# A two-layer latent backbone on one core: five instead of four tiles of the input projection multiplied while their input is still being made

## The chip, the core and the metric

The kernel runs on one core of a Trainium2 chip. Its engines each take their instructions in the order in which they stand in the program: PE (the matrix engine, with PEld for its weight loads), DVE (vector), ACT (scalar), POOL, and SP, which here only issues transfers. The metric is the time of one execution in microseconds, smaller is better. Results of PE go to PSUM, which has eight banks of 128 x 512 numbers; everything else lies in SBUF or, through transfers, in DRAM.

## What is computed

Two layers over 256 context tokens and 256 latent tokens, 1024 wide. What matters here is the start of the first layer: both streams are modulated (scaled and shifted by two vectors that come out of a product of the condition with `mod_w`), and the result goes through one wide projection `w_in`. Part of its output, `rw`, is mixed with its neighbours in time and feeds a recurrent scan.

```python
for l in range(DEPTH):
    sh1, sc1, g1, sh2, sc2, g2 = split((silu(c) @ mod_w[l] + mod_b[l]), 6)
    cq, ckv, kr, ch, cb, cc, rw, gt = split(modulate(x, sh1, sc1) @ w_in[l], IN_SPLITS)
    ...
    # rwkv_features: part is rw
    part = part + (0.5 * (up[:, :-2] + up[:, 2:]) - part) * mu
    r, k, v, wd, ad, gd = split(part, ...)
    kk = kkf * rsqrt(max(sum(square(kkf)), 1e-24))     # kkf = heads(k * k_k)
    ...
    # scan over the tokens, both directions; attention; gated merge; FFN
```

## The kernel before

Each product in full precision is made of three matmuls on split operands (`mm3`, L238 to L240: high by high, high by low, low by high), 128 x 512 each. Since the inner size is 1024, one output tile of `w_in` (128 features by all 512 tokens) takes 8 x 3 = 24 matmuls and one PSUM bank. `w_in` has 57 such tiles. Fifteen of them are the `rw` part, here called tiles 0 to 14: 0 and 1 feed the decay and the learning rate of the scan, 2 to 5 are its keys.

`start` makes the modulated input of the first layer in eight pieces k = 0 to 7 (one for each 128 of the 1024 channels): it loads `mod_w`, multiplies it (`mod`, L259, and `mod_out`, L266, into the banks `p_m`), transposes x (L1295, bank `p_i`), scales and shifts on DVE (L1299) and splits into `xh` and `xl` (ACT and DVE, L245 and L246). While the pieces come, the first `M_START` tiles of `w_in` are already multiplied. Tile m is loaded and split (`wload`, L193 and L194) at piece m, catches up on pieces 0 to m, and then takes part in each later piece. Tiles 0 and 1 use the two banks `pg`, the others the banks `p_w`:

```python
if k < M_START:
    ws.append(wload(A["win"][0, M_RW + k], [128, 8, 128], pl=ip, tag="w", nb=4 * M_START))
    acc.append(pg() if k < 2 else pr("w", M_START - 2))
...
for m in range(len(ws)):
    for kk in range(k + 1) if m == k else (k,):
        mm3(acc[m], ws[m][0](kk), ws[m][1](kk), xh[:, kk], xl[:, kk], kk == 0, kk == 7)
```

When piece 7 is done, `feature(m, acc[m])` takes each tile out of its bank: ACT copies it to `pp` (L480), POOL adds the neighbours into `nb` (L483), ACT scales `pp` (L484), DVE combines both (L485), and SP stores `nb` to DRAM as `feat` (L491). `pp` and `nb` share a ring of four buffers. Tiles 0 and 1 are then loaded again for the scan (`tw`, L967) and split on ACT (`wa`, L245). The later tiles are multiplied one after the other by `gemm_in` into three banks in turn and taken out the same way. The four key tiles are loaded back as `kn` (L537, through the same ring of four buffers), squared on ACT (L937), and summed on PE (`p_y<-bones,kn`, L945).

The program is written in one order and a scheduler in the language's framework then reorders the instructions of every engine before the kernel is built. The order that each engine gets is fixed from then on. So a change in one place may move instructions elsewhere.

Of the kernel before, what the change touches and what calls it, by code (L numbers as in the profile page):

```python
# [46 lines left out]
R_WD, R_AD, R_K, R_R, R_V, R_GD = 0, 1, 2, 6, 10, 14  # L47
NM_IN = 57

M_START = 4  # L50
N_EARLY = (24, 24)
N_CONV = (2, 1)
BC = 4
# [23 lines left out]
def body(ctx: ExitStack, tc: tile.TileContext, A: dict, out: bass.AP, dbg=None, upto=None):  # L77
# [12 lines left out]
    def pg():  # L90

        if extra[0]:
            extra[1] = (extra[1] + 1) % (extra[0] + 2)
            if extra[1] < extra[0]:
                return psp[0].tile([128, 512], F32, tag="x", name="pg", bufs=extra[0])
        return psg.tile([128, 512], F32, tag="g", name="pg")

    def pr(tag, bufs=1):
        return psp[0].tile([128, 512], F32, tag=tag, name="p_" + tag, bufs=bufs)
# [76 lines left out]
    def wload(src, shape, pl=None, tag=None, nb=None, to=None):  # L176

        w, n = shape[-1], int(np.prod(shape[1:]))
        raw = ring.tile([128, 1024], F32, tag="raw", name="raw", bufs=3)
        sp.dma_start(out=raw[:, :n].rearrange("p (a b) -> p a b", b=w), in_=src)  # L180
        his, los = [], []
        for i, o in enumerate(range(0, n, 512)):
            m = min(512, n - o)
            if to:
                hi, lo = (t[:, o:o + m] for t in to)
            else:
                p = pl or ring
                hi = p.tile([128, 512], F32R, tag=tag or "hi", name="hi", bufs=nb or 4)[:, 0:m]
                lo = p.tile([128, 512], F32R, tag=tag or "lo", name="lo", bufs=nb or 4)[:, 0:m]
            r = raw[:, o:o + m]  # L190
            cnt[0] += 1
            e = pool if share[0] and cnt[0] % share[0] == 0 else dve
            act.copy(out=hi, in_=r)  # L193
            e.tensor_tensor(out=lo, in0=r, in1=hi.bitcast(F32), op=ALU.subtract)  # L194
            his.append(hi)
            los.append(lo)

        def part(ts):
            return lambda k: ts[k * w // 512][:, k * w % 512:k * w % 512 + w]

        return part(his), part(los)
# [35 lines left out]
    def mm3(ps, wh, wl, xh, xl, first, last):  # L237
        pe.matmul(ps, wh, xh, start=first, stop=False, skip_group_check=True)  # L238
        pe.matmul(ps, wh, xl, start=False, stop=False, skip_group_check=True)  # L239
        pe.matmul(ps, wl, xh, start=False, stop=last, skip_group_check=True)  # L240

    def split(src, hi, lo, scale=None):

        if scale is None:
            act.copy(out=hi, in_=src)  # L245
            dve.tensor_tensor(out=lo, in0=src, in1=hi.bitcast(F32), op=ALU.subtract)  # L246
        else:
            act.mul(out=hi, in_=src, mul=scale)
            dve.scalar_tensor_tensor(out=lo, in0=src, scalar=scale, in1=hi.bitcast(F32), op0=ALU.mult,
                                     op1=ALU.subtract)  # L250
# [197 lines left out]
    def layer(l, xh=None, xl=None, pre=()):  # L448
# [16 lines left out]
        with ExitStack() as rws:  # L465
# [42 lines left out]
            if l == 0:  # L508
                xh, xl = start(feature)
                m0 = M_START  # L510
            rp = rws.enter_context(tc.tile_pool(name=f"rw{l}", reuse_waits="tile", bufs=1))
# [760 lines left out]
    def start(feature):  # L1272

        xh, xl = new_xm()
        with tc.tile_pool(name="ini", bufs=1, reuse_waits="tile") as ip, banks("psi"):
# [9 lines left out]
            for k in range(8):  # L1285
# [15 lines left out]
                split(xf, xh[:, k], xl[:, k])  # L1301
# [3 lines that stand above are left out]
                if k == X_AT:  # L1305
# [5 lines left out]
# [3 lines that stand above are left out]
            for m in range(M_START):  # L1314
                feature(m, acc[m])
# [78 lines left out]
```

## Time and profile before

| | |
|---|---|
| time, three runs | 1870.13, 1872.61, 1875.64 us; median 1872.61 us |
| the profiled execution | 1882.8 us, of which its span 1881.0 us |
| granted TensorE clock over the span | 0.969 |
| PE busy | 1795.3 us (95%), 13556 instructions |
| DVE / ACT / POOL busy | 1087.1 / 842.4 / 547.3 us |
| transfers | 380.45 MB, mean 202 GB/s |

The profile lists each instruction with its start, its length and, in brackets, how long its engine had been idle before it and which instruction ended that wait. Matmuls overlap each other by their filling and draining, so the distance from one start to the next, not the length, is what one costs. "Granted clock" is the share of TensorE's full clock (2.4 GHz) that the chip gave; 0.5 is 1.2 GHz.

### The profile page before, as it was taken

To read this page: it belongs to the slowest core of one execution; us is meant where nothing else is said; L and a number is where in the kernel's file an instruction comes from. 1 tells how busy PE (TensorE), PEld (TensorE's weight loads), DVE (VectorE), ACT (ScalarE), POOL (GpSimd) and SP (SyncE) were. 2 spreads that over 40 slices of the span, in tenths; PEclk is the share of its full clock that TensorE was granted. 3 is DMA by queue.
4 is the path that set the end of the run, shared out by engine and by line. 5 is a ranking of instruction groups with operands and counts; after the bars stand their busy time and mean duration, and the time that the engine had idled before them with its cause. 6 is when DMAs were issued, how large, how long until landed. Compare 5 with 4: busy or idle time off the path is not lost.

```text
span 1881.0 us, 35386 instructions
## 1 busy us (share of the span) xinstructions
PE 1795.3 (95%) x13556; PEld 1477.6 (79%) x13556; DVE 1087.1 (58%) x2012; ACT 842.4 (45%) x1830; POOL 547.3 (29%) x558
## 2 busy tenths in 40 slices
PE   7999999999989998999999998999999999989997
PEld 5777877777768767877888887777788886869996
DVE  4357724873367787543444346168874368855665
ACT  2557333823245453444444213386523365535552
POOL 1356113611133221454343015244302132420001
PEclk9998999999989999999999999988899999989999
DMA  8443534343495326799999425775586573576573
GB/s 339 135 143 107 163 131 155 105 156 124 166 313 161 120 74 217 261 370 345 344 335 357 134 89 177 236 233 157 177 262 212 185 267 121 175 289 225 182 240 106
DMA packets 182698, 380.45 MB, mean 202 GB/s; under 512 B 33984, under 2 KB 89344, under 8 KB 182528
## 3 DMA queue, kind: packets, MB, share of 16 engines
q1 hardware_dynamic: 179552, 369.59, 58.1%
q10 hardware_dynamic: 2976, 8.59, 1.3%
q8 instruction: 107, 1.75, 0.4%
q14 instruction: 63, 0.52, 0.1%
HBM read 301.53 MB, written 76.58 MB: 201 GB/s over the span
## 4 chain that ended last, share of the span: by engine, by line
PE 73%; DVE 9%; DMA 9%; ACT 5%; issue 3%; POOL 1%; SPq 0%; ACTq 0%; POOLq 0%; DVEq 0%
PE pg L238 10%; PE pg L239 10%; PE pg L240 10%; PE p_f L238 9%; PE p_f L240 9%; PE p_f L239 8%; DMA raw<-in_win_dram 3%; PE p_G L1066 2%; PE p_G L755 2%; DVE lo L194 1%; PE pg L259 1%; PE p_y L776 1%; ACT hi L193 1%; DMA raw<-in_ffn_w_dram 1%; DVE sq L1106 1%
## 5 line engine op out<-in xcount | busy, mean ns | idle before, releaser
L194 DVE TENSOR_TENSOR lo<-raw,hi 128x512 fp32r<-128x512 f32 (+1 forms) x408 | 317.1, 787 | 361.8 <-ACT hi L193 358.5
L193 ACT CAST hi<-raw 128x512 fp32r<-128x512 f32 x478 | 286.5, 616 | 424.6 <-PE p_f L239 97.0
L238 PE MATMUL pg<-xh,hi 128*128 128x512 f32 (+1 forms) x912 | 335.7, 370 | 12.1 <-ACT pp L480 3.7
L240 PE MATMUL pg<-xh,lo 128*128 128x512 f32 (+1 forms) x912 | 329.4, 361 | 0.2
L239 PE MATMUL pg<-xl,hi 128*128 128x512 f32 (+1 forms) x912 | 327.8, 359 | 0.4 <-DVE xl L246 0.4
L238 PE MATMUL p_f<-x2h,hi 128*128 128x256 f32 (+1 forms) x688 | 232.9, 338 | 7.2 <-ACT hi L193 7.2
L240 PE MATMUL p_f<-x2h,lo 128*128 128x256 f32 (+1 forms) x688 | 231.9, 337 | 1.1 <-DVE lo L194 1.0
L239 PE MATMUL p_f<-x2l,hi 128*128 128x256 f32 (+1 forms) x688 | 231.5, 336 | 0.0
L238 PEld LDWEIGHTS pg<-xh,hi 128*128 128x128 f32 x912 | 180.2, 198 | 45.3 <-issue 9.1
L240 PEld LDWEIGHTS pg<-xh,lo 128*128 128x128 f32 x912 | 180.7, 198 | 25.8 <-issue 2.0
L239 PEld LDWEIGHTS pg<-xl,hi 128*128 128x128 f32 x912 | 180.8, 198 | 21.9 <-DVE xl L246 1.0
L194 POOL TENSOR_TENSOR lo<-raw,hi 128x512 fp32r<-128x512 f32 x70 | 93.2, 1331 | 343.2 <-ACT hi L193 306.5
L238 PEld LDWEIGHTS p_f<-x2h,hi 128*128 128x128 f32 x688 | 131.5, 191 | 22.5 <-ACT hi L193 9.4
L240 PEld LDWEIGHTS p_f<-x2h,lo 128*128 128x128 f32 x688 | 131.4, 191 | 15.8 <-DVE lo L194 2.6
L239 PEld LDWEIGHTS p_f<-x2l,hi 128*128 128x128 f32 x688 | 131.5, 191 | 12.7
L231 POOL TENSOR_TENSOR wlo<-wraw,whi 128x512 fp32r<-128x512 f32 x70 | 92.7, 1345 | 123.7 <-ACT whi L230 123.5
L334 POOL TENSOR_TENSOR rs<-rs,mhalf 128x1 f32<-128x1 f32 x12 | 8.8, 730 | 352.8 <-DVE rs L353 352.8
L1050 POOL TENSOR_TENSOR FM<-ta,di 64x256 f32<-64x256 f32 x64 | 57.4, 897 | 37.3 <-ACT FM L1044 21.6
L661 POOL TENSOR_TENSOR acc<-acc,gts 128x512 f32<-128x512 f32 (+1 forms) x32 | 38.7, 1217 | 79.9 <-DVE gts L659 67.3
L259 PE MATMUL pg<-raw,cs 128*32 128x128 f32 x1024 | 53.7, 299 | 2.0 <-DMA raw<-in_modw_dram 1.7
L1106 DVE TENSOR_TENSOR sq<-sq,iv 128x31 f32<-128x31 f32 (+15 forms) x124 | 50.6, 408 | 3.4
L1066 PE MATMUL p_G<-AR,FM 64*128 64x128 f32 x384 | 51.0, 290 | 1.1 <-DVE AR L1074 1.0
(393 smaller groups left out, 3599.2 us busy)
## 6 DMA issues: line engine op xcount, KB each, us to landing
raw<-in_modw_dram SPq DMA_DIRECT2D x96, 512.0 KB, 4.8
raw<-in_w_dram SPq DMA_DIRECT2D x88, 512.0 KB, 5.2
raw<-in_win_dram SPq DMA_DIRECT2D x79, 512.0 KB, 4.3
raw<-in_ffn_w_dram SPq DMA_DIRECT2D x44, 512.0 KB, 3.7
wraw<-in_win_dram SPq DMA_DIRECT2D x35, 512.0 KB, 6.1
win<-whi SPq DMA_DIRECT2D x35, 512.0 KB, 5.8
win<-wlo SPq DMA_DIRECT2D x35, 512.0 KB, 5.3
hi<-win SPq DMA_DIRECT2D x70, 256.0 KB, 4.0
```

The source lines that it names most:

```text
L193: act.copy(out=hi, in_=r)
L194: e.tensor_tensor(out=lo, in0=r, in1=hi.bitcast(F32), op=ALU.subtract)
L231: pool.tensor_tensor(out=lo[:, s], in0=raw[:, s], in1=hi[:, s].bitcast(F32), op=ALU.subtract)
L238: pe.matmul(ps, wh, xh, start=first, stop=False, skip_group_check=True)
L239: pe.matmul(ps, wh, xl, start=False, stop=False, skip_group_check=True)
L240: pe.matmul(ps, wl, xh, start=False, stop=last, skip_group_check=True)
L259: pe.matmul(ps[32 * (k % 4):32 * (k % 4) + 32, 0:128], cs[:, o:o + 32], raw[:, k], start=(j == 0 and k < 4), stop=(k >= 4), skip_group_che ...
L661: pool.tensor_tensor(out=a, in0=a, in1=g, op=ALU.add)
L755: pe.matmul(ps[:, 0:nk], qT[:, h, qt * 128:(qt + 1) * 128], kT[:, h, 0:nk], start=True, stop=True)
L1050: pool.tensor_tensor(out=FM[r, :, k0:k0 + 64], in0=rc(ta[r]), in1=rc(Pi[r]), op=ALU.mult)
L1066: pe.matmul(ps[:, j * 128:j * 128 + ncol], FM[r, j], AR[z][r, e, hp, j, 0:ncol], start=True, stop=True)
L1106: dve.tensor_tensor(out=Ti[:, j + 1:32, 0:w], in0=Ti[:, j + 1:32, 0:w], in1=tv, op=ALU.subtract)
```

## The change

One constant is raised, which makes `start` load, split and multiply tile 4 at piece 4 as well. Its accumulator is a third `p_w` bank, so that all eight banks are taken in `start` (two `pg`, two `p_m`, one `p_i`, three `p_w`). The weights' ring in `start` grows from 16 to 20 buffers, and `gemm_in` has one tile fewer to do.

```diff
-M_START = 4
+M_START = 5
```

The set of instructions stays the same: all engines run as many of each kind as before, and only one copy out of PSUM reads a `p_w` instead of a `pg` bank. The order does change. Every engine's order differs in many places in the mixers of the first layer, in a few in its feed-forward part and at the start of the second layer, and then not at all.

The first place is on PE, in piece 4. `pg_310`, `pg_367`, `p_w_424` and `p_w_487` are the banks of tiles 0 to 3, `p_m` those of the modulation. Before, the last tile's matmuls are followed by the modulation of the next piece, and then piece 5 begins:

```order
L239 MATMUL p_w_487<-xl_253,hi_483 128x512
L240 MATMUL p_w_487<-xh_252,lo_484 128x512
L266 MATMUL p_m_558<-pick_78,modrow_579 128x4
L259 MATMUL p_m_607<-raw_608,cs_77 32x128 x5
L259 MATMUL p_m_607<-raw_618,cs_77 32x128 x8
L259 MATMUL p_m_656<-raw_657,cs_77 32x128 x8
```

Now tile 4 (`p_w_556`) catches up there; of its fifteen matmuls the first three and the last three are shown:

```order
L240 MATMUL p_w_487<-xh_252,lo_484 128x512
L238 MATMUL p_w_556<-xh_252,hi_548 128x512
L239 MATMUL p_w_556<-xl_253,hi_548 128x512
L240 MATMUL p_w_556<-xh_252,lo_549 128x512
...
L238 MATMUL p_w_556<-xh_252,hi_552 128x512
L239 MATMUL p_w_556<-xl_253,hi_552 128x512
L240 MATMUL p_w_556<-xh_252,lo_553 128x512
L266 MATMUL p_m_584<-pick_78,modrow_605 128x4
```

Fifteen matmuls moved ahead of the modulation of pieces 5 to 7, and three more go into each of these pieces.

The second place is on ACT, where the first tiles of `gemm_in` leave PSUM. `pp_838`, `pp_881` and `pp_964` belong to tiles 5, 6 and 7, the four `kn` to the key tiles, and `tw`, `di` and `PC` to the scan's decay. Before:

```order
L484 ACTIVATE pp_838<-pp_838,hv0_83 128x2x256
L480 COPY pp_881<-pg_856 128x2x256
L1026 ACTIVATE tw_1323<-tw_1323,ones_70 128x256
L193 CAST hi_1024<-raw_1022 128x512
L1030 ACT_TABLE_LOAD
L1030 ACTIVATE di_1329<-tw_1323 128x256
L484 ACTIVATE pp_881<-pp_881,hv0_83 128x2x256
L1031 ACTIVATE tw_1323<-tw_1323 128x256
L1032 COPY PC_1298<-tw_1323 128x4
L193 CAST hi_1028<-raw_1022 128x512
L937 ACTIVATE kn_889<-kn_889,sv_74 128x2x256
L937 ACTIVATE kn_902<-kn_902,sv_74 128x2x256
```

Now:

```order
L484 ACTIVATE pp_838<-pp_838,hv0_83 128x2x256
L480 COPY pp_881<-pg_856 128x2x256
L193 CAST hi_1028<-raw_1022 128x512
L484 ACTIVATE pp_881<-pp_881,hv0_83 128x2x256
L937 ACTIVATE kn_889<-kn_889,sv_74 128x2x256
L937 ACTIVATE kn_902<-kn_902,sv_74 128x2x256
L193 CAST hi_1067<-raw_1065 128x512
L193 CAST hi_1071<-raw_1065 128x512
L937 ACTIVATE kn_911<-kn_911,sv_74 128x2x256
L937 ACTIVATE kn_920<-kn_920,sv_74 128x2x256
L480 COPY pp_964<-pg_939 128x2x256
```

The decay's instructions went behind the keys' squares; tile 7 still leaves its bank behind all four squares. On PE the first sum over a key tile (L945) stands, before, behind 121 matmuls of `gemm_in` and six small ones (`p_c<-wa,uhl`) counted from the end of `start`; now behind 100 and three.

The third place is on PE at the end of the first layer's mixers, where the last pieces of the modulation (L259, L266) are made between the scan's read-out (L1233 and L1248 are transposes, L1267 the read-out's gate) and the merge (`pg<-br,hi`). Before:

```order
L1233 MATMUL p_y<-ident,Yf 128x128 x4
L266 MATMUL pg<-pick,modrow 128x4
L1267 MATMUL p_G<-sg,lw 128x256
L276 MATMUL pg<-ident,modT_81 16x128
L259 MATMUL pg<-raw,cs 32x128 x24
L266 MATMUL pg<-pick,modrow 128x4
L259 MATMUL pg<-raw,cs 32x128 x16
L266 MATMUL pg<-pick,modrow 128x4
L1248 MATMUL p_y<-ident,gn 128x128 x4
L259 MATMUL pg<-raw,cs 32x128 x8
L1233 MATMUL p_y<-ident,Yf 128x128 x4
L1267 MATMUL p_G<-sg,lw 128x256
```

Now:

```order
L259 MATMUL pg<-raw,cs 32x128 x16
L1248 MATMUL p_y<-ident,gn 128x128 x4
L259 MATMUL pg<-raw,cs 32x128 x8
L266 MATMUL pg<-pick,modrow 128x4
L1233 MATMUL p_y<-ident,Yf 128x128 x4
L259 MATMUL pg<-raw,cs 32x128 x8
L266 MATMUL pg<-pick,modrow 128x4 x2
L259 MATMUL pg<-raw,cs 32x128 x16
L266 MATMUL pg<-pick,modrow 128x4
L238 MATMUL pg<-br,hi 128x512
```

Between the last tile of `gemm_in` and the merge there stand one L1248 group, one L1233 group and two L1267 fewer than before; they come later, among the merge's matmuls.

## Rows read from the trace of the kernel before

**Rows 1.** Stretches: length; busy (count) PE, PEld, DVE, ACT, POOL; PEclk; DMA share; GB/s.

```profile
30.00:43.76 13.76, 13.51 (x120) 9.72 (x119) 8.14 (x16) 4.99 (x10) 2.71 (x2) 1.00 0.81 317
43.76:55.47 11.71, 11.71 (x110) 9.96 (x108) 6.07 (x18) 2.98 (x6) 0.44 (x1) 1.00 0.22 59
...
93.00:100.00 7.00, 6.93 (x28) 5.72 (x29) 4.11 (x5) 2.98 (x6) 5.60 (x6) 0.76 0.17 47
```

**Rows 2.** PE in order of time: start, length, instruction.

```profile
43.76 0.28 PE L266 MATMUL p_m<-pick,modrow 128*128 128x4 f32 x2
...
55.47 0.39 PE L238 MATMUL pg<-xh,hi 128*128 128x512 f32 x1
...
60.91 0.39 PE L238 MATMUL pg<-xh,hi 128*128 128x512 f32 x1
...
71.88 0.38 PE L238 MATMUL p_c<-wa,uhl 64*128 64x256 f32 x1
...
72.78 0.50 PE L238 MATMUL pg<-xh,hi 128*128 128x512 f32 x1
```

**Rows 3.** Chain that ended last: start, us, what.

```profile
58.30 2.54 DMA feat<-nb
60.86 2.18 DMA tw<-feat
...
64.90 2.44 DMA feat<-nb
67.36 1.99 DMA tw<-feat
...
71.23 4.69 DMA feat<-nb
...
79.52 4.12 DMA kn<-feat
...
83.66 0.73 ACT kn L937
```

**Rows 4.** ACT in order of time.

```profile
54.36 0.59 ACT L480 COPY pp<-pg 128x512 f32<-128x512 f32 x1 [2.53 <-PE pg L240]
...
92.43 0.59 ACT L480 COPY pp<-pg 128x512 f32<-128x512 f32 x1 [1.31 <-POOL pp L479]
```

**Rows 5.** PE in order of time, around the keys' sums.

```profile
84.44 1.05 PE L945 MATMUL p_y<-bones,kn 128*128 128x2 f32 x8 [0.26 <-ACT kn L937]
...
93.06 0.79 PE L238 MATMUL pg<-xh,hi 128*128 128x512 f32 x1 [1.29 <-ACT pp L480]
...
96.22 0.49 PE L239 MATMUL pg<-xl,hi 128*128 128x512 f32 x1
```

**Rows 6.** Transfer issues: count, KB each, median us to landing.

```profile
feat<-nb SPq DMA_DIRECT2D x25, 256.0 KB, 3.1
...
kn<-feat SPq DMA_DIRECT2D x4, 256.0 KB, 4.1
```

**Rows 7.** PE in order of time, later waits of the first layer.

```profile
248.11 0.44 PE L1188 MATMUL p_c<-Zs,LB 64*64 64x64 f32 x2 [2.54 <-ACT LB L1138]
...
536.79 1.12 PE L1233 MATMUL p_y<-ident,Yf 128*128 128x128 f32 x4 [2.13 <-ACT Yf L1251]
...
550.01 1.12 PE L1233 MATMUL p_y<-ident,Yf 128*128 128x128 f32 x4 [0.58 <-ACT Yf L1251]
```

**Rows 8.** Stretches around those waits, columns as in rows 1.

```profile
241.00:250.00 9.00, 6.46 (x151) 4.92 (x153) 1.07 (x2) 5.72 (x11) 1.26 (x1) 0.81 0.34 119
250.00:259.00 9.00, 9.00 (x72) 6.71 (x64) 2.24 (x4) 2.49 (x6) 0.00 (x0) 0.81 0.42 147
...
536.00:542.00 6.00, 4.63 (x57) 3.31 (x57) 3.33 (x8) 3.16 (x9) 0.00 (x0) 0.72 0.83 266
542.00:548.00 6.00, 3.61 (x40) 2.62 (x40) 2.43 (x7) 1.43 (x5) 1.98 (x1) 0.63 0.98 370
548.00:554.00 6.00, 5.42 (x44) 3.63 (x43) 3.85 (x9) 3.36 (x9) 1.52 (x2) 0.52 1.03 381
```

## The prediction

> **What bounds the kernel now.** I first read the stretches of the start, because the change moves work into it. From 43.76 us, where the fifth tile is put in, to 55.47 us PE is busy for all of the 11.71 us, and in the 13.76 us before it for all but 0.25 [rows 1]. Next I read PE in order of time: the matmuls of tile 4 now begin at 55.47, right behind the last matmul of `start`, and end at 60.91 where tile 5 begins [rows 2]. So PE has no hole there, neither where the tile goes to nor where it is taken from. Transfers are no limit in that stretch (DMA share 0.22 [rows 1]), and the load of tile 4's weights stands at the same place of SP's queue as before.
>
> Then the chain that ended last, read from 58 to 85 us. It doesn't run over PE there: tile 0 is stored to DRAM (2.54 us) and read back (2.18), tile 1 stored (2.44) and read back (1.99), tile 3 stored (4.69), and the first key tile read back (4.12), with short pieces of ACT and DVE between [rows 3]. It begins with the copy of tile 0 out of its bank at 54.36 [rows 4] and ends in the square at 83.66, which the first sum over a key tile waits for on PE. That sum starts at 84.44, after a wait of 0.26 us [rows 5]: chain and PE arrive together. Then PE waits 1.29 us at 93.06 for tile 7 to leave its bank [rows 5], and runs slow for a while.
>
> **The change, part by part.** *The matmuls.* Tile 4 has 24 matmuls; 60.91 - 55.47 = 5.44 us, 0.227 each [rows 2]. They leave one full stretch and enter another, so they gain 0. (TensorE: Matmul & The Clock Gate of the Trainium skill, section "Wait — 56ns, not 53.3ns?", gives 215.7 ns for such a matmul at the full clock; the trace's 0.227 is 5% above it. If all of that were room to be had, it would be 24 x 0.011 = 0.3 us of an estimate, no term here.) The two casts and two subtractions of tile 4's weights were already made in piece 5 before, so ACT and DVE only have those of tile 6 more there, in time that PE's fifteen extra matmuls cover (DVE is busy for 6.07 of 11.71 us, ACT for 2.98 [rows 1]). The fifth bank costs nothing: the next user of that bank is the scan, after 100 us.
>
> *Tile 0 leaves later.* Between 43.76 and tile 0's last matmul PE now does 15 matmuls in piece 4, 3 each in pieces 5 and 6, and 1 in piece 7: 22 x 0.227 = 5.0 us. The copy at 54.36 [rows 4] comes at 59.4, and with it the whole chain of stores and loads, since it is made of latencies and not of PE's work. Left alone it would bring the first squared key 5.0 us later, ready at 84.4 + 5.0 = 89.4.
>
> *PE comes just as early.* By the order the first key sum stands behind 100 matmuls of `gemm_in` and 3 small ones, counted from the end of `start`, which comes at 60.91 now. 100 x 0.227 = 22.7, and half of the 0.90 us between 71.88 and 72.78 that six small ones take [rows 2], make 84.05. Before, it came at 84.18. So the key sum, which waited 0.26 us, would wait up to 5.3. How much of the 5.0 the chain makes up is not in the trace, so I bound it: if the store of 4.69 and the load of 4.12 [rows 3] both took the 2.2 us of the short reloads, it would save 4.4, and the wait is 1.0; if nothing, 5.3. I take the middle by the medians: the store's is 3.1 and the key load's is 4.1 [rows 6], so only the store becomes shorter, by 1.6. The wait becomes 84.4 + 5.0 - 1.6 - 84.05 = 3.7 us. Behind that sum on PE stand tiles 9 and 10, with their operands ready; nobody can pass.
>
> DMA: Bandwidth & Descriptors of the Trainium skill, section "Anatomy of one DMA — SWDGE (gpsimd) path", puts a transfer at some 2.0 us plus its bytes over 436 GB/s. For 256 KB that is an estimate of 2.6 us; the stores of 2.54 and 2.44 agree with it, the 4.69 and the 4.12 do not [rows 3]. By it both long ones would be 2.6, the chain would make up 3.6, and the sum below would be 0.4 instead of 2.4. I go by the medians.
>
> *The clock after the wait.* From 93.06 to 96.22 seven matmuls took 3.16 us instead of 1.59 [rows 5], after a wait of 1.29; the granted clock from 93 to 100 was 0.76 [rows 1], so it stood at 1.2 GHz part of the time. A wait of 3.7 should do the same: 1.6 us. Bounds: 0, and what followed the wait of 2.54 at 248 us [rows 7], two stretches of 9 us at 0.81 [rows 8], which is 2 x 1.7 = 3.4.
>
> *The wait at 93.06 goes.* It was for the copy of tile 7 (92.43 [rows 4]), whose clearing stood behind other work of POOL. That work is ordered later now, and PE comes later as well (84.05 + 3.7 + 0.8 for the sum + 4.5 for 20 matmuls + 1.6 + 0.8 = 95.5). The copy ended at 92.43 + 0.59 = 93.0, of which 1.31 was the wait for POOL [rows 4]; without that wait and with the chain's delay it ends by 93.0 - 1.3 + 5.0 - 1.6 = 95.1. So 1.29 + 1.57 = 2.9 us are given back; bounds 0 and 2.9.
>
> *The rest of the first layer's order.* Nothing in it is longer or shorter, but waits can come and go. I found one place that bears on the time, from 530 to 554 us, where the last modulation pieces run at a DMA share of 0.83 to 1.03 and granted clocks of 0.72, 0.63 and 0.52 [rows 8]. Four small pieces of read-out have left it for the full stretch behind it. If the transfers set its length, they cost their own time: four at half of 1.12 us [rows 7], 2.2. If the waits for the read-out there (2.13 and 0.58 [rows 7]) go, 2.7 is gained. I take 0 between them.
>
> **Sum.** 0 + 3.7 + 1.6 - 2.9 + 0 = +2.4 us, on the profiled execution 1882.8 + 2.4 = 1885.2. That execution lies 10.2 above the median of the three runs, so for the median: 1872.6 + 2.4 = 1875.0. The bounds add to 1.0 + 0 - 2.9 - 2.7 = -4.6 and 5.3 + 3.4 + 0 + 2.2 = +10.9.
>
> **The rivals.** *Slower.* The key chain makes up nothing and tile 7's bank is late as well. The price is 5.3 + 3.4 with nothing given back, +8.7: 1881. It decides if the first key's load lands later than 88 us. For it speaks that in the order weight loads of 512 KB still stand on SP's queue among these stores; against it that the one which stood just ahead of the first key's load now stands behind it.
>
> *Faster.* The read-out's pieces no longer stop PE between 530 and 554 us, so that the clock stays up. The waits of 2.7 and the half-clock losses of 6 x (0.28 + 0.37 + 0.48) = 6.8 [rows 8] are 9.5 us; with the 2.4 it is -7.1: 1865.5. For it speaks the third place of the order, against it the DMA share of 1, which leaves PE nothing to do faster.
>
> *It fills holes after all.* If PE's 5.44 us were hidden in waits of `start`, the time would be 1867.2. The busy 11.71 of 11.71 speaks against it, and I give it little.
>
> *It does nothing.* The chain makes up enough for the key's wait to equal what the wait at 93.06 gives back: 1872.6.
>
> **How the numbers follow.** My forecast has 0.43, nothing 0.14, slower 0.25, faster 0.15, filled holes 0.03. A measurement can tell 0.3%, 5.6 us, from no change: the forecast and nothing are within it (0.57, and 1869 to 1878 is the forecast's own range), slower by more has 0.25, faster by more 0.18. The range reaches to 1865 and 1885: the bounds of the sum, and nearly all of the two rivals.
>
> **What would show it.** In the changed profile PE should run without a hole from 43.8 to 60.9, tile 0 should be copied at about 59.4, the first key sum should start at about 88 after a wait of 3 to 4 us, with matmuls of 0.43 behind it, and the wait at 93 should be gone. I am wrong if the key sum waits under 1 us, if the wait for tile 7's copy stays, or if PE's waits between 120 and 560 us change by more than 4 us in total.

## The result, and the profile after

The change makes the kernel slower: the median goes from 1871.37 us (four runs, 1869.04 to 1875.64) to 1890.79 us (four runs, 1889.68 to 1897.15), a ratio of 1.0104 [1.0076, 1.0133] (in brackets, here and below, the 95% interval). Ratios leave out executions that took over 1.5% longer than the fastest of the same kernel; that concerns two of e8's twelve below and no others, and with them the means of e8 and of before have the ratio 0.9986. The profiled execution took 1897.15 us; its span is 14.3 us longer than that of before. Lines of the changed kernel's page: each engine's busy time, the granted clock in 40 equal slices of the span (in tenths; the second such line is that of before), and the two groups of transfers of [rows 6]:

```profile
PE 1802.5 (95%) x13556; PEld 1480.9 (78%) x13556; DVE 1087.1 (57%) x2012; ACT 842.1 (44%) x1830; POOL 547.4 (29%) x558
...
PEclk9999999998979999999999999988889999989999
...
PEclk9998999999989999999999999988899999989999
...
feat<-nb SPq DMA_DIRECT2D x25, 256.0 KB, 2.9
...
kn<-feat SPq DMA_DIRECT2D x4, 256.0 KB, 3.1
```

PE runs as many instructions as before and is busy 7.2 us longer, so some of them ran at a lower clock; the other 7 us are idle time. The first low digits of the clock stand in the tenth slice (426 to 474 us) and the twelfth (521 to 569), far behind `start`; before, they stand in the fourth (141 to 188) and the twelfth.

First the start, which the prediction was mostly about. Stretches of the changed kernel, columns as in [rows 1]:

```profile
43.76:60.91 17.15, 17.15 (x132) 14.25 (x131) 6.58 (x19) 2.88 (x6) 0.20 (x1) 1.00 0.26 80
60.91:93.00 32.09, 29.62 (x134) 23.97 (x133) 12.15 (x15) 15.99 (x28) 15.68 (x25) 1.00 0.49 155
93.00:100.00 7.00, 6.04 (x33) 5.09 (x31) 1.37 (x3) 3.47 (x6) 4.46 (x4) 1.00 0.52 172
```

PE in order of time, the places of [rows 5] and the first of [rows 7], and the wait at 79.82:

```profile
79.82 0.50 PE L238 MATMUL pg<-xh,hi 128*128 128x512 f32 x1 [1.19 <-ACT pp L480]
...
87.78 1.05 PE L945 MATMUL p_y<-bones,kn 128*128 128x2 f32 x8 [1.28 <-ACT kn L937]
...
95.26 0.50 PE L238 MATMUL pg<-xh,hi 128*128 128x512 f32 x1 [0.96 <-ACT pp L480]
...
246.03 0.44 PE L1188 MATMUL p_c<-Zs,LB 64*64 64x64 f32 x2 [3.74 <-ACT LB L1138]
```

ACT, the copy that answers to the first of [rows 4]:

```profile
60.05 0.59 ACT L480 COPY pp<-pg 128x512 f32<-128x512 f32 x1 [3.44 <-PE pg L240]
```

The chain that ended last, its stores and its key load. Here it runs on past the first key sum, so its last two transfers belong to a later key:

```profile
63.99 2.53 DMA feat<-nb
...
70.72 2.65 DMA feat<-nb
...
82.84 2.77 DMA feat<-nb
...
86.91 4.03 DMA feat<-nb
...
90.95 3.04 DMA kn<-feat
```

PE has no hole from 43.76 to 60.91. The first key sum comes at 87.78 instead of 84.44, the last one at 105.45 instead of 104.11. So the start costs 1.3 us by then, and the rest of the loss comes later. To find where, I compared when the same piece of the program begins in both traces. The scan's products with `LB` (L1188) begin at 246.03 in its first half (248.11 before, so the start's loss is made good) and at 439.31 in its second (437.64 before: +1.7). The attention's 16 products (L776), at 687.72 before, begin at 700.95: +13.2. The first transposes of the feed-forward part (L315), at 735.89 before, begin at 751.00: +15.1.

Most of it falls around the second half of the scan (a second place, from 530 to 566 us, is shown further below). The stretch from 405 to 475 us, in the changed kernel:

```profile
405.00:475.00 70.00, 64.89 (x756) 50.37 (x754) 29.65 (x52) 21.05 (x37) 9.54 (x11) 0.88 0.31 102
...
435.00:440.00 5.00, 3.36 (x142) 2.82 (x144) 2.67 (x4) 3.23 (x6) 1.27 (x1) 0.90 0.15 32
440.00:445.00 5.00, 5.00 (x43) 3.14 (x35) 0.13 (x1) 1.25 (x3) 0.00 (x0) 0.50 0.75 284
445.00:450.00 5.00, 5.00 (x24) 3.75 (x25) 0.86 (x2) 0.59 (x1) 0.00 (x0) 0.50 0.01 5
450.00:455.00 5.00, 5.00 (x19) 3.37 (x18) 1.36 (x3) 1.24 (x2) 0.00 (x0) 0.73 0.00 0
```

and in the kernel before:

```profile
405.00:475.00 70.00, 67.81 (x876) 54.29 (x873) 33.46 (x64) 24.35 (x43) 12.33 (x12) 1.00 0.39 132
```

Idle time is 5.1 instead of 2.2 us, and the clock 0.88 instead of 1.00, which is 0.12 x 70 = 8.4 us: 11.3 in all. Two waits at 411.90 and 413.89 (1.86 and 1.61 us; before has two of 1.38 and 0.80) and a clock of 0.88 from 411 to 425 us are the smaller part of it. After a wait that ends at 439.31, TensorE had 1.2 GHz for all of the ten microseconds from 440 to 450, though PE was busy throughout. PE and ACT around that wait, changed kernel:

```profile
435.12 2.21 PE L1134 MATMUL p_G<-LB,sq 32*32 32x32 f32 x128
...
439.31 0.45 PE L1188 MATMUL p_c<-Zs,LB 64*64 64x64 f32 x2 [1.64 <-ACT LB L1138]
...
435.79 1.14 ACT L193 CAST hi<-raw 128x512 fp32r<-128x512 f32 x2 [2.65 <-DMA raw<-in_win_dram]
437.83 0.72 ACT L597 ACTIVATE hs<-u,sv 128x512 f32<-128x512 f32 x1 [0.90 <-DVE u L596]
438.58 2.42 ACT L1138 ACTIVATE LB<-p_G 32x512 f32<-32x512 f32 x4
```

and before:

```profile
435.49 2.21 PE L1134 MATMUL p_G<-LB,sq 32*32 32x32 f32 x128
437.64 0.33 PE L1188 MATMUL p_c<-Zs,LB 64*64 64x64 f32 x2
...
436.74 2.42 ACT L1138 ACTIVATE LB<-p_G 32x512 f32<-32x512 f32 x4 [2.51 <-PE p_G L1134]
439.19 0.62 ACT L193 CAST hi<-raw 128x512 fp32r<-128x512 f32 x1
439.98 0.72 ACT L597 ACTIVATE hs<-u,sv 128x512 f32<-128x512 f32 x1 [0.18 <-DVE modT L291]
```

The four copies L1138 take the scan's powers out of PSUM, and L1188 needs them. Before, ACT stood ready for them. Now two casts of a weight (L193) and one step of an output (L597) stand ahead of them on ACT. The casts waited 2.65 us for the weight's transfer and L597 0.90 us for DVE, and the copies began at 438.58, though L1134 had already filled their first bank. (TensorE: Matmul & The Clock Gate of the Trainium skill, section "Architectural detail: the array is 16× 32×32, not 1× 128×128", says that ACT takes its queue strictly in order; this trace agrees, since the copies began only after L597.)

### The profile page after: what moved, and what is told of

Same layout as the page of the kernel before. It is cut to its first block, busy times and chain, and to the rows that moved or that the text cites. A ratio compares the mean times of both kernels' runs of the same rounds, so it can differ in the third digit from the quotient of the medians.

```text
span 1895.3 us, 35381 instructions
## 1 busy us (share of the span) xinstructions
PE 1802.5 (95%) x13556; PEld 1480.9 (78%) x13556; DVE 1087.1 (57%) x2012; ACT 842.1 (44%) x1830; POOL 547.4 (29%) x558
## 4 chain that ended last, share of the span: by engine, by line
PE 72%; DMA 10%; DVE 9%; ACT 4%; issue 4%; POOL 1%; SPq 0%; ACTq 0%; POOLq 0%; DVEq 0%
PE pg L238 10%; PE pg L239 9%; PE pg L240 9%; PE p_f L238 9%; PE p_f L240 9%; PE p_f L239 9%; DMA raw<-in_win_dram 3%; PE p_G L1066 2%; PE pg L259 2%; DVE lo L194 1%; PE p_G L755 1%; ACT hi L193 1%; DMA raw<-in_modw_dram 1%; PE p_y L776 1%; DMA raw<-in_ffn_w_dram 1%
## 5 line engine op out<-in xcount | busy, mean ns | idle before, releaser
L194 DVE TENSOR_TENSOR lo<-raw,hi 128x512 fp32r<-128x512 f32 (+1 forms) x408 | 317.0, 787 | 363.4 <-ACT hi L193 350.7
L193 ACT CAST hi<-raw 128x512 fp32r<-128x512 f32 x478 | 286.6, 616 | 442.3 <-PE pg L239 93.4
L238 PE MATMUL pg<-xh,hi 128*128 128x512 f32 (+1 forms) x904 | 331.7, 369 | 10.8 <-DMA hi<-win 3.2
L240 PE MATMUL pg<-xh,lo 128*128 128x512 f32 (+1 forms) x904 | 325.5, 360 | 0.8 <-DMA lo<-win 0.7
L194 POOL TENSOR_TENSOR lo<-raw,hi 128x512 fp32r<-128x512 f32 x70 | 93.0, 1329 | 323.8 <-ACT hi L193 279.5
L259 PE MATMUL pg<-raw,cs 128*32 128x128 f32 x1024 | 57.3, 310 | 8.1 <-DMA raw<-in_modw_dram 7.5
L259 PEld LDWEIGHTS pg<-raw,cs 128*32 128x32 f32 x1024 | 30.7, 119 | 26.6 <-DMA raw<-in_modw_dram 9.1
```

The costliest lines, as they stand in the source:

```text
L259: pe.matmul(ps[32 * (k % 4):32 * (k % 4) + 32, 0:128], cs[:, o:o + 32], raw[:, k], start=(j == 0 and k < 4), stop=(k >= 4), skip_group_che ...
```

## Experiments

**Theory.** The loss is not the fifth tile but the order that the scheduler made of the rest of the first layer: short waits in the scan, each followed by a stretch at 1.2 GHz. **Rivals:** the late start itself (tile 0, the transfers and the fifth bank), and some single transfer that comes late.

Several kernels hold an order: when the program has been traced, each instruction of an engine is made to stand behind the one that stood ahead of it in another kernel's order. These added dependencies carry no wait of their own; no run holds a kernel's own order unaltered, so it is not shown that holding is free. All ratios are to the kernel before on the same chip, five rounds each.

**e1 and e2: the change's parts apart.** `gemm_in` takes three shared banks in turn, dealt by a counter in `pg()`:

```
if extra[0]:
    extra[1] = (extra[1] + 1) % (extra[0] + 2)
    if extra[1] < extra[0]:
        return psp[0].tile([128, 512], F32, tag="x", ...)
return psg.tile([128, 512], F32, tag="g", ...)
```

The fifth accumulator of `start` doesn't count there, so every later tile gets another bank than before; I call this the turn. e1 has five tiles, the old turn, and on PE, behind `start`, the order of before. e2 has four tiles, the change's turn and PE's order of the change.

```diff
 e1
-M_START = 4
+M_START = 5
-    extra = [0, 0]
+    extra = [0, 1]
...
+        pin(tc)     # PE: order of before
 e2
-    extra = [0, 0]
+    extra = [0, 2]
...
+        pin(tc)     # PE: order of the change
```

> Five tiles at the start, as in the change, but behind the first 288 matmuls (those of the start and of all five tiles) TensorE's instructions stand in the order of the kernel before, and the mixers' accumulators take the three shared banks in the turn of before. Order theory (the loss came from the order of the first layer's rest, which changed with the start): it is gone, and what stays is the start's own lag of 1.3 to 2.4 us, so 1872 to 1875 us, and no wait of over 1 us with TensorE at half clock between 405 and 460 us. Start theory (the fifth tile itself, by the later features and what follows from them): as slow as the change, 1888 to 1893 us.

> Four tiles at the start, as before the change, but behind the first 288 matmuls TensorE's instructions stand in the order of the changed kernel, with its turn of the banks. Order theory: as slow as the changed kernel or little faster, 1886 to 1891 us, with waits of over 1 us and half clock between 405 and 460 us. Start theory: the time of before, 1869 to 1874 us.

Measured: e1 1878.31 us, 1.001 [0.9993, 1.0026]; e2 1900.5 us, 1.0132 [1.0108, 1.0155]. Five tiles in the old order cost nothing that can be told, four tiles in the new order cost more than the change. By the ratios the order theory holds; in microseconds both lie above what it foretold (e1 by some 3, e2 by some 10), and before itself took 1874.9 us on that chip. In e1 the first key sum comes 7.3 us later than before (91.75), held by

```profile
76.69 0.58 PE L238 MATMUL p_c<-wa,uhl 64*128 64x256 f32 x1 [2.84 <-ACT wa L245]
```

and yet L315 begins at 736.8, only 0.9 us later. The delay is 4.2 us at the last key sum (108.31), 1.7 at the scan's L1178 (209.16 against 207.43), and 0.9 at L1188: the kernel before was held up on the way itself, with a clock of 0.89 from 92 to 108 us and 0.88 from 180 to 215, where e1 had 1.00 and 0.95. The stretch from 405 to 475 us in e1,

```profile
405.00:475.00 70.00, 67.89 (x887) 54.20 (x876) 33.48 (x65) 24.09 (x43) 12.32 (x12) 1.00 0.42 135
```

and in e2,

```profile
405.00:475.00 70.00, 62.74 (x706) 48.56 (x705) 31.06 (x56) 21.67 (x38) 9.53 (x11) 0.90 0.33 109
```

follows the order, not the number of tiles.

**e3, e4, e12, e13: the turn of the banks alone, with the scheduler free.** `M_START` and the start value of the turn are all that differs:

```diff
 e3
-M_START = 4
+M_START = 5
-    extra = [0, 0]
+    extra = [0, 1]
 e12
+M_START = 5
+    extra = [0, 2]
 e4
+    extra = [0, 2]
 e13
+    extra = [0, 1]
```

> Five tiles at the start; only the turn of the three banks that the mixers' accumulators share is set on by one, so that each later accumulator has the bank that it has before. The scheduler orders the rest; its order of TensorE's instructions comes back to that of before at the 3217th matmul of 10,492 (with the change alone, at the 6141st). Order theory with the bank's turn behind it: most of the loss is gone, 1868 to 1880 us. Order theory without it (any other order costs as much): 1880 to 1891 us. Start theory: 1888 to 1893 us.

> Four tiles at the start as before, and the turn of the three shared banks set as the change leaves it for the tiles from the sixth on. Order theory with the bank's turn behind it: slower than before, 1880 to 1892 us. Order theory without it: anywhere between 1866 and 1892 us. Start theory: the time of before, 1869 to 1874 us.

> Five tiles, and the turn of the three shared banks set on by two: neither the turn of before nor that of the change. If the loss belongs to the one turn that the change brings: near before or near the run with five tiles and the old turn, 0.998 to 1.007. If any order other than that of before loses about as much: 1.004 to 1.012. If the start is what counts: 1.009 to 1.012.

> Four tiles, and the turn of the three shared banks set on by one, so that the order of the first layer is planned anew with no other change. If any order other than that of before loses: 1.004 to 1.012. If it is the change's turn alone: 0.997 to 1.003.

| ratio to before | old turn | the change's turn | third turn |
|---|---|---|---|
| four tiles | 1 | 1.0075 [1.0052, 1.0099] (e4) | 0.9976 [0.9953, 0.9998] (e13) |
| five tiles | 1.0059 [1.0034, 1.0084] (e3) | 1.0104 [1.0076, 1.0133] | 1.0021 [0.9997, 1.0045] (e12) |

Without a fifth tile, the turn alone moves the time by +0.75% or -0.24%. Within a turn, five tiles are 0.59, 0.29 and 0.45% slower than four, known to 0.25, 0.37 and 0.33%, so the middle one is not told from nothing. e3 (1885.63 us) lies above the 1868 to 1880 foretold for the turn alone, and e13 shows that not every other order loses. So, as an estimate, some half of the change's 1.04% (0.45, undone in e3, to 0.75, made in e4) comes with the turn that the fifth tile shifts. The rest comes with the tile and the other re-ordering that it sets off; by e1 the tile itself is little of it, by e11 (below) it may be more. In the third turn the second half has no wait at all. In e13:

```profile
405.00:475.00 70.00, 70.00 (x1037) 56.22 (x1037) 32.87 (x55) 25.30 (x45) 12.82 (x13) 1.00 0.39 122
```

**e5 and e6: the copies ahead, in the change.** All engines hold the change's order, but for ACT. In e5 the four copies go ahead of L597 in the scan's second half; in e6 also ahead of two casts and of L585 in its first half:

```
e5, second half          e6, first half (and e5's edit)
 L193 CAST hi<-raw x2    -L193 CAST hi<-raw x2
+L1138 LB<-p_G x4        -L585 ACTIVATE gt<-pg
 L597 hs<-u,sv            L1138 LB<-p_G x4
-L1138 LB<-p_G x4        +L193 CAST hi<-raw x2
                         +L585 ACTIVATE gt<-pg
```

> The changed kernel with every engine's order held as it is, but for one instruction: on ScalarE the activation of a gate's convolution (L597, 0.72 us, which waits for VectorE) stands behind the four copies into LB (L1138) in the second half of the scan, and no longer ahead of them. Place theory (what costs there is that the copies come late, and the half clock that follows TensorE's wait): the wait of 1.64 us at 439.31 and most of the half clock from 439 to 453 us go, 1.6 + 6 = some 7 us, ratio to before about 1.0065 where the change has 1.0104. Rival (the clock fell because of the waits at 411.90 and 413.89, or the matmuls of L1188 wait for something else then): only the wait or nothing, 0 to 2 us, ratio 1.0095 to 1.0105.

> As the run before it, and also in the first half of the scan: the two casts of a weight (L193) and the activation of a gate (L585), which stand ahead of the copies into LB (L1138) on ScalarE, stand behind them. Place theory: there goes also most of the wait of 3.74 us at 246.03 and the half clock behind it until 251.5 us, 5 to 6 us more: ratio to before about 1.003. Rival (the casts are missed as much as the copies are gained): no faster than the run before it.

Measured: e5 1888.9 us, 1.0091 [1.0058, 1.0125]; e6 1887.97 us, 1.0079 [1.0048, 1.011]. Neither differs from the change by more than its interval, and both missed the place theory's 1.0065 and 1.003. PE and ACT of e5 in the second half, and then the ten microseconds behind L1188:

```profile
444.01 0.30 PE L1188 MATMUL p_c<-Zs,LB 64*64 64x64 f32 x2 [0.18 <-ACT LB L1138]
...
442.12 1.14 ACT L193 CAST hi<-raw 128x512 fp32r<-128x512 f32 x2 [2.92 <-DMA raw<-in_win_dram]
443.28 2.42 ACT L1138 ACTIVATE LB<-p_G 32x512 f32<-32x512 f32 x4
```

and

```profile
445.00:450.00 5.00, 5.00 (x47) 3.53 (x45) 2.22 (x4) 2.27 (x5) 0.00 (x0) 1.00 0.85 306
450.00:455.00 5.00, 5.00 (x45) 3.62 (x45) 2.12 (x4) 1.24 (x2) 0.00 (x0) 1.00 0.02 8
```

Where L1188 waits 0.18 us instead of 1.64, the clock behind it stays at 1.00 (it was 0.50 behind L1188 in the change), so in this execution one edit takes the wait and the low clock away together. But the casts still stand ahead, so the arrival of their weight decides: in e6 the same second half waited again,

```profile
433.98 0.44 PE L1188 MATMUL p_c<-Zs,LB 64*64 64x64 f32 x2 [1.55 <-ACT LB L1138]
```

In e6's first half, where the casts went behind as well, the wait is gone: L1188 begins there at 243.2 and needs nobody.

**e7 and e8: the same edit on before, and a spliced order.** e7 is the kernel before, its order held, with one cast moved behind the copies in the first half. e8 has four tiles, e4's order and turn on PE up to matmul 898 and before's from there (one step of the turn skipped), and e7's move:

```diff
 e7, order of ACT
-L193 CAST hi<-raw
 L1138 LB<-p_G x4
+L193 CAST hi<-raw
 e8
-    extra = [0, 0]
+    extra = [0, 2, 0]
...
+            extra[2] += 1
-            extra[1] = (extra[1] + 1) % (extra[0] + 2)
+            extra[1] = (extra[1] + 1 + (extra[2] == 26)) % (extra[0] + 2)
```

> The kernel before with every engine's order held, but for one instruction: the cast of a weight (L193, 0.62 us) that waits for its transfer until 246.74 us stands behind the four copies into LB (L1138) in the first half of the scan. Place theory: the wait of 2.54 us at 248.11 and the half clock behind it until 253.9 us go for the most part, 2 to 5 us: ratio to before 0.9973 to 0.999. Rival (the gap is filled by a wait for that weight or taken up by the next wait): 1.000.

> Four tiles at the start; up to the 898th matmul TensorE's order and the banks' turn are those of the run with four tiles and the new turn, from there on those of the kernel before (one step of the turn is skipped at the 26th accumulator), and the cast of the run before this one stands behind the copies into LB. In the run whose first part it takes, TensorE was 10.8 us ahead of before at 200 us, since it lacks the wait at 179.30 and the half clock behind it. If each part of the order is worth by itself what it showed there: 8 to 14 us faster than before, ratio 0.9925 to 0.9957. If the lead is taken up by the next common wait, as the lag of the first experiment's start was between 180 and 260 us: 0.997 to 1.000.

Measured: e7 1865.36 us, 0.9971 [0.9948, 0.9994]; e8 1867.18 us, 0.9967 [0.9944, 0.9991]. In e7 the wait of 2.54 [rows 7] and the slow stretches around it [rows 8] are gone. PE in order of time, and the two stretches:

```profile
244.26 0.32 PE L1188 MATMUL p_c<-Zs,LB 64*64 64x64 f32 x2
```

```profile
241.00:250.00 9.00, 9.00 (x198) 6.99 (x197) 2.21 (x4) 6.42 (x12) 1.27 (x1) 1.00 0.63 203
250.00:259.00 9.00, 9.00 (x106) 7.25 (x105) 2.75 (x4) 2.28 (x5) 2.32 (x2) 1.00 0.50 155
```

By [rows 8] these 18 us held 2.54 us of idle time and 2 x 1.7 lost to the clock, 5.9 in all; e7 is 0.29% or 5.4 us faster, by its interval 1 to 10 us. e8's spliced part was to add to that and added nothing that can be told. Its last group of 16 products L1066 before L1178 comes 9.6 us earlier than before's (186.73 against 196.35), and then PE waits for the load of v:

```profile
203.19 0.44 PE L1178 MATMUL p_c<-SV,AR 128*64 128x64 f32 x2 [6.20 <-DMA SV<-vtm]
```

**e9, e10, e11: the casts too, the change again, five tiles with both.** e9 is the change with the casts behind the copies in both halves; e10 is the change unaltered; e11 is e1 with e7's move.

```
e9, second half           e9, first half
+L1138 LB<-p_G x4         as in e6
 L193 CAST hi<-raw x2
 L597 hs<-u,sv            e11: e1's diff and
-L1138 LB<-p_G x4         e7's move on ACT
```

> The changed kernel with every engine's order held, but on ScalarE the four copies into LB (L1138) stand ahead of both casts of a weight (L193) and of the gate's activation (L585 in the first half of the scan, L597 in the second) in both halves. In the run before it that left the casts ahead in the second half, these waited for their transfer at 432 us and the wait of 1.55 us and the half clock stayed. Place theory: both waits of L1188 under 0.6 us and the clock full from 440 to 460 us; of the change's loss some 13 of 19 us are regained, ratio to before 1.002 to 1.005, and what is left lies between 655 and 760 us. Rival (in another execution another instruction is the late one): 1.007 to 1.010.

> The change once more, on the same chip as the run before this and the one behind it, so that their ratios can be set beside it: 1.008 to 1.013.

> Five tiles with TensorE's order of before behind the start, as in the first experiment, and the cast behind the copies into LB as in the run with four tiles that was faster (ratio 0.9971). If the fifth tile itself costs no more than the 1.3 to 2.4 us of the start: 0.997 to 0.999, faster than both kernels. If the first experiment hid the start's lag of some 4 us in the wait at 248 us, which is now gone: 0.9985 to 1.0005.

Measured: e9 1888.79 us, 1.0077 [1.005, 1.0105]; e10 1890.79 us, 1.0108 [1.0071, 1.0146]; e11 1873.0 us, 1.0008 [0.9984, 1.0032]. e11 lies above both of its forecasts. It is 0.37% slower than e7, to some 0.33%, and in its profile the second L1188 begins 3.2 us later than e7's (434.44 against 431.24). So part of the fifth tile's lag was hidden in e1 by waits that before has as well (at the first L1188 2.54 us before, 1.72 in e1), and shows where that wait is gone. e10 shows the costly place again: L1188 waits 2.50 us at 443.73, and the clock is 0.50 from 445 to 455. e9 missed most of what I expected. In its second half the copies come in time, and then the next thing is late:

```profile
432.40 0.33 PE L1188 MATMUL p_c<-Zs,LB 64*64 64x64 f32 x2
...
435.62 0.65 PE L259 MATMUL pg<-raw,cs 128*32 128x128 f32 x16 [2.54 <-DVE u L596]
...
434.27 0.69 DVE L194 TENSOR_TENSOR lo<-raw,hi 128x512 fp32r<-128x512 f32 x1 [6.99 <-ACT hi L193]
434.88 0.68 DVE L596 TENSOR_TENSOR u<-pg,hs 128x512 f32<-128x512 f32 x1
```

The modulation's L259 needs a bank that L596 empties on DVE, and L596 stands behind a subtraction (L194) that needs the cast, which now comes behind the copies. The wait moved from 1.64 to 2.54 us and the clock fell as before (0.88 from 405 to 475).

**e14 and e15: u moved too; the two gains together.** e14 is e9 with L596 ahead of the two subtractions. e15 is e13 with its casts and L585 behind the copies in the first half.

```
e14, DVE: e9 and     e15, ACT: e13 and
-L194 lo x2          -L585 gt<-pg, L193 x2
 L596 u<-pg,hs        L1138 LB<-p_G x4
+L194 lo x2          +L585 gt<-pg, L193 x2
```

> As the run with the copies first in both halves, and on VectorE the product u of a gate's convolution (L596), on whose bank the modulation's matmuls (L259) waited for 2.54 us at 435.62, stands ahead of the two subtractions (L194) that wait for the late weight. If that was the wait that took the place of the one removed: no wait of over 1.3 us between 430 and 440 us, no half clock from 436 to 447 us, 4 to 7 us less than that run in this stretch, ratio to before 1.003 to 1.005. If the weight itself is what comes too late there: a wait of 1 to 2.5 us for it, and 1.006 to 1.008 as before.

> Four tiles with the third turn of the banks, every engine's order held as in that run, but in the first half of the scan the gate's activation (L585) and the two casts of a weight (L193) stand behind the four copies into LB (L1138) on ScalarE, as in the run with four tiles and the cast moved. There TensorE waited 3.1 us for these copies. If the two gains add: 3 to 6 us less than that run, ratio to before 0.994 to 0.996. If another wait takes its place: 0.997 to 0.998.

Measured: e14 1878.35 us, 1.0029 [1.0004, 1.0053]; e15 1871.77 us, 1.0005 [0.998, 1.0029]. e14 came as foretold: PE has no wait from 425 to 450 us, and the clock stays up. PE, and the stretch from 405 to 475 us:

```profile
434.93 0.32 PE L1188 MATMUL p_c<-Zs,LB 64*64 64x64 f32 x2
```

```profile
405.00:475.00 70.00, 66.36 (x875) 52.49 (x874) 33.97 (x60) 23.66 (x42) 10.48 (x11) 0.98 0.38 121
```

From 1.0106 (the change, mean of its two ratios) through 1.0077 (e9) to 1.0029: to put the copies ahead of four casts and two other steps on ACT, and L596 ahead of two subtractions on DVE, gives back some three quarters of the loss. Five tiles, the change's turn and PE's order are kept. e15 was a miss: what e13 and e7 gain does not add, and a new wait stands behind the repaired one:

```profile
248.00 0.33 PE L1194 MATMUL p_c<-SV,TM 128*64 128x64 f32 x2 [1.68 <-ACT SV L1189]
```

Where three places of the program begin on PE in the profiled executions (us), beside the ratio:

| | L1188, first half | L1188, second half | L315 | ratio |
|---|---|---|---|---|
| before | 248.1 | 437.6 | 735.9 | 1 |
| the change | 246.0 | 439.3 | 751.0 | 1.0104 |
| e10, again | 248.9 | 443.7 | 753.6 | 1.0108 |
| e1 | 249.0 | 438.0 | 736.8 | 1.001 |
| e2 | 249.6 | 445.3 | 752.9 | 1.0132 |
| e9 | 242.8 | 432.4 | 744.3 | 1.0077 |
| e14 | 245.6 | 434.9 | 739.9 | 1.0029 |
| e7 | 244.3 | 431.2 | 727.8 | 0.9971 |
| e13 | 238.9 | 420.3 | 728.6 | 0.9976 |

From the second L1188 to L315 before's order takes 298.3 us, e1 298.8, e7 296.6; the change 311.7, e9 311.9, e14 305.0. That stretch holds the change's loss, and e14 halves it; in e10 and e2 another 6 and 8 us are lost ahead of it. The second L1188 nearly sorts all the profiled executions: in the change, e10, e2, e3, e4 and e6 it waits 1.55 to 2.50 us, and their ratios are 1.0059 to 1.0132; in before, e1, e7, e8 and e11 to e15 it does not wait, and theirs are 0.9967 to 1.0029. The exceptions are e9, whose wait moved to L259, and e5 (0.18 us, 1.0091); why e5's repair did not show in its time stays open.

## Why the prediction was wrong

**The matmuls and tile 0: right.** PE is full from 43.76 to 60.91, so the tile fills no holes, and tile 0 is copied at 60.05 (foretold 59.4).

**The wait at the first key sum: the place right, the size wrong.** It starts at 87.78, foretold at about 88, but after a wait of 1.28 us, not 3.7. PE itself came later: a tile's copy held it for 1.19 us at 79.82, which the count of matmuls left out, and `gemm_in` began at 61.61, not 60.91. Since the end of the wait was right, its term was nearly right as a delay. The key load's median became 3.1 us on the page, not 4.1, so more was made up than I took: tile 0's copy came 5.7 us later and the first key's square 3.3 (87.00 against 83.66), which is 2.4 and not 1.6. My lower bound for the wait was taken from the reloads `tw`, which move 128 KB and not the 256 KB of a key tile. (DMA: Bandwidth & Descriptors of the Trainium skill, section "Anatomy of one DMA — SWDGE (gpsimd) path", gave the estimate of 2.6, but fits transfers that GpSimd issues, and SP issues these: the stores of 2.53, 2.65 and 2.77 agree, the store of 4.03 and the load of 3.04 don't.)

**The clock after it (+1.6) and tile 7's wait (-2.9): both off.** After waits of 1.19 and 1.28 us the granted clock was 1.00 from 60.91 to 100, so the first is 0. Tile 7's wait remains at 0.96, so that of the second only 0.3 came with the wait and 1.6 with the clock, which was 0.76 there [rows 1]. Together the start costs 1.3 us at the last key sum, against my sum of 2.4. The start was foretold to about a microsecond, partly by luck: the key sum's delay was put 0.4 too high, the clock 1.6 too high, and what tile 7's wait gives back 1.0 too high.

**"The rest of the first layer's order ... I take 0": the step that failed.** Its bounds were -2.7 to +2.2, and the change lost some 14 us there in the profiled execution (15.1 at L315, less the start's 1.3). I had looked at one place, from 530 to 554 us, where the difference between the orders was plain to see, and priced only the waits that stood in the trace of before. That place alone lost 3.7 us, beyond my 2.2 (see the rivals). The costlier one was another, the second half of the scan: there before has no wait because ACT stands ready when a bank is full, and in the new order it does not. e2, with the start unchanged and only PE's order and the turn taken from the change, shows that these can cost as much without a fifth tile, 1.0132; the other engines' order is the scheduler's own there. e1, with PE's order unchanged, has 1.001 against my 1.0013, but e11 shows that part of its lag lay hidden in before's own waits, so this agreement is partly luck.

**My own signs of error.** Of the three, the first did not come (the key sum waited over 1 us), and the second did (tile 7's copy is still waited for, 0.96 us). The third: PE's idle time from 120 to 560 us went from 13.6 to 17.6 us, which is the 4 that I had named as the limit; its clock there went from 0.96 to 0.95, about another 4. Waits alone would have told half of it. That stretch before,

```profile
120.00:560.00 440.00, 426.40 (x4022) 332.51 (x4021) 255.93 (x475) 202.47 (x476) 140.75 (x152) 0.96 0.47 154
```

and in the changed kernel:

```profile
120.00:560.00 440.00, 422.38 (x3992) 329.00 (x3990) 252.97 (x458) 198.57 (x468) 131.55 (x146) 0.95 0.46 150
```

**The rivals.** The slower one (+8.7 in the start) did not happen; the loss came by another way. The faster one did not either. From 530 to 554 us alone PE is idle for 4.1 instead of 6.2 us and the clock is 0.81 instead of 0.72, but the slow stretch lasts longer: the merge begins at 561.48 instead of 554.65, and the clock is 0.50 until 565. From 530 to 566 us, before and then in the changed kernel:

```profile
530.00:566.00 36.00, 29.84 (x258) 22.28 (x257) 23.07 (x49) 16.76 (x38) 12.77 (x13) 0.81 0.88 308
...
530.00:566.00 36.00, 29.34 (x260) 21.14 (x259) 17.64 (x36) 15.35 (x34) 8.45 (x9) 0.72 0.85 297
```

Idle time and the low clock together take 6.2 + 6.8 = 13.0 us of it before and 6.7 + 10.1 = 16.7 in the change, so this place adds 3.7 us to the loss. PE still waits there for the modulation's transfer (2.78 us at 545.61).

**What stays open.** How the fifth tile's own cost splits: e1 puts it at 0.1%, e11 beside e7 at 0.4%, the pairs within a turn at 0.3 to 0.6%, and these contain re-ordering. Where e14's last 0.3% lies: in its one profile the stretch from the second L1188 to L315 is 6.7 us longer than before's, of which 2.8 fall between 530 and 566 us (PE idle 5.7 us, clock 0.72), and no run undoes that. Why the gains of e13 and e7 do not add. And whether e7, e8 or e13 would hold their 0.3% beyond these runs: their intervals end within 0.1% of 1.

## What to carry to other kernels

Where a scheduler reorders the program, a small edit changes two things: the work that it moves, and the order of all that follows; cost the second by holding the old order and running both halves apart. On an engine that takes its instructions in order, an instruction that waits for a late transfer holds everything behind it: put what PE waits for ahead of casts of weights that are still on their way, and then look who is late next, on the other engines too. A wait of one or two microseconds in a full matrix engine can cost several more through the clock (1.64 us at 439.31 was followed by some 6 us lost to it, 1.28 us at 87.78 by none), so count the waits that an order creates and not only those that it removes.

## What the runs showed of the hardware

Some short waits were followed by the lower clock and some were not. In the changed kernel the wait of 1.64 us at 439.31, behind 128 matmuls of 32 x 32, was followed by 1.2 GHz for over ten microseconds of full work. Before, the wait of 1.29 us at 93.06 among full 128 x 512 matmuls was followed by a granted clock of 0.76 from 93 to 100 us [rows 5, rows 1]. Waits of 1.19, 1.28 and 0.96 us among such matmuls in the changed kernel (79.82, 87.78, 95.26) left it at 2.4 GHz. No run varied the wait or the matmuls around it alone, so what decides is not shown.

The wait at one place differs between executions of one order. L1188's first wait was 3.74 us in the change and 4.83 in e10, the same kernel:

```profile
248.91 0.45 PE L1188 MATMUL p_c<-Zs,LB 64*64 64x64 f32 x2 [4.83 <-ACT LB L1138]
```

From L315 to the end of the span, where the change left the order mostly as it was, single executions took from 1129.3 us (e1) to 1147.1 us (e9); before took 1145.1 and the change 1144.3. This is more than the start's whole effect, so the single profile tells where the time goes, and only the repeated runs how much.
